# Two value row blocks placed behind the first scores, later divisions by the last sums, casts of outputs in other half heads, and an earlier table request, in a two-layer encoder on one core

## The chip, the cores and the metric

The program runs on one core of one Trainium2 chip. The metric is the device time of one execution in microseconds (us). A core has one queue of instructions for each engine: TensorE (PE, matrix products; PEld is its weight load), VectorE (DVE), ScalarE (ACT), GpSimd (POOL) and SyncE (SP, which only issues DMA transfers). Each engine works through its own queue in order, and a semaphore holds an instruction until what it needs is there.

## The reference, cut to what matters

Two layers, 1,024 positions, 1,024 channels. Each layer joins 8-head latent attention (512 channels) and a convolution branch (512 channels), multiplies both by `w_o`, adds the residual, and then runs a gated feed-forward part with a 3-tap convolution.

```
def _mla_attention(q_nope, q_rope, k_nope, k_rope, v):
    ...
        sc = (jnp.einsum("bqhd,bkhd->bhqk", qn, k_nope)
              + jnp.einsum("bqhr,bkr->bhqk", qr, k_rope))
        p = jax.nn.softmax(sc.astype(jnp.float32) * scale, axis=-1).astype(v.dtype)
        return jnp.einsum("bhqk,bkhd->bqhd", p, v)
...
        kv = (c_kv @ w_ukv[l].astype(h.dtype)).reshape(b, s, MLA_HEADS, MLA_NOPE_DIM + MLA_V_DIM)
        v = kv[..., MLA_NOPE_DIM:]
        y_attn = _mla_attention(q_nope, q_rope, k_nope, k_rope, v)
        ...
        u = jax.nn.silu(_layernorm(u, g_conv_ln[l], b_conv_ln[l]))
        y = jnp.concatenate([y_attn, u], axis=-1) @ w_o[l].astype(h.dtype)
        x = x + y
```

The change touches the attention of each layer: how `v` is made at its start, and how the outputs of the heads are divided by the softmax's sums, split and multiplied by `w_o` at its end.

## The kernel before, in words

Numbers that need more than half precision are kept as a high and a low half (names ending in h and l), and a product is three products of halves. `attention` (L1821) runs once in each layer. Its work comes in **pairs**: 8 heads x 8 blocks of 128 queries, two blocks to a pair, 32 pairs in a layer, numbered 0 to 31. In a name such as `s_0_2` the first number is the head, the second the query block; `t_7_22` is head 7, pair 2 of that head, column group 2.

- **Values.** `rows(tt)` (L1830) makes row block `tt` (0 to 7) of `v`: six matmuls into one PSUM bank `pv`, then `rows_end` (L1839): two ACT copies and two DVE operations that write the high and the low half. Before the loop, the kernel makes blocks 0 to 3 (`ROWS_FIRST`), then the first scores, then 4 and 5, then 6 and 7.
- **Scores.** `scores` (L1851) makes the two score tiles of a pair: four matmuls of the first tile, four short ones with the rotary part `kq` for both, four of the second. `again` (L2051) copies the rotary queries once more, for those short matmuls; it runs once for each head.
- **Softmax.** `largest` (L1875, DVE) takes the negative maximum `mx` of a score tile; `expo` (L1882, ACT) takes the exponential `p` and its sum. Its first call loads a function table (ACT_TABLE_LOAD) that the operations ahead of it did not need.
- **Turning.** `turn` (L1898) transposes `p` on PE in four groups of 4 matmuls, each into a bank `t`; `upper` (L1912, ACT) and `lower` (L1915, DVE) write the high and low half, `pt`.
- **Outputs.** `values` (L1919) and `values_end` (L1935) multiply `pt` by `v` into a bank `o`, two pairs (a half head) at a time; ACT and DVE add the two halves of `o` into `yt`. Pairs with an even number hold `values`' part with 6 matmuls, odd ones the end of a half head.

PSUM has two wide tiles for scores (and for `po_e`) and four banks that `pv`, `t`, `o` and `rc` share, so that a matmul group waits until an older tile's last reader is done. In the loop each pair writes the next pair's scores between the transposes of this one, so PE, ACT and DVE go round in one cycle.

An **agenda** holds side work by its time in half pairs: `others(n)` (L2038) runs what is due. `sums(h)` (L1955) inverts a head's sums, writes them to memory (`sd`) and reads them back spread over the partitions (`rb`); POOL multiplies `yt` by `rb`, and `ys.append(self.split(...))` then casts the product to `ys_1h`, `ys_3h`, `ys_5h` on ACT (a CAST of 128x1024) and makes the low half on POOL. `SUMS_AT`, `Y_DELAY`, `Y_SPLIT` and `Y_LAST` are these times. For the last head the sums are inverted on DVE (`inverse`, L1973) and spread by four transposes on PE into a bank `rc_0s` or `rc_1s` (`spread`, L1978), and DVE divides (L1981). Head 6's outputs are multiplied by `rb` on DVE, in two parts at the times `LAST_MULT`.

At the end of the attention the first products with `w_o` are made early: `early(0, ...)` (L1984) is nine matmuls `po_e` over three pairs of heads, in the order high x high, low x high, high x low. The weights `wo` are loaded by POOL's DMA queue (L1002); `complete` (the dictionary `ahead`, L989) writes the high half of one block on ACT (128x512), and POOL then issues a DMA that forms its low half (L214), 256 KB each. Beside this, POOL adds up the convolution for the layer norm (`lns`, L2173), and SP's queue holds the loads of the residual `y`, issued behind the sums' transfers.

Of the kernel before, what the change touches and what calls it, by code (L numbers as in the profile page):

```python
# [64 lines left out]
FFN_BANKS = (2, 4)  # L65
SIDE_TIME = 56
TOTAL_TIME = 57
Y_DELAY = 5
SUMS_AT = 8
Y_LAST = 4  # L70
Y_SPLIT = 8
LATE_FROM = 0
LAST_MULT = (61, 62)
WO_AT = 55
END_TURNS = 1
SCALES_AT = 2, 4.2
# [3 lines left out]
WO_LOWER = (3, 4), (4, 2), (5, 2), (6, 2)  # L80
P_SCALE = 32768.0
EXPONENT = 8388608.0
ROWS_FIRST, ROWS_SECOND, ROWS_THIRD = (0, 1, 2, 3), (4, 5), (6, 7)
# [66 lines left out]
class Encoder:  # L150
# [421 lines left out]
    def project(self, l, carry):  # L572
# [229 lines left out]
        def query(j):  # L802
            n = self.blk(f"qn{l}_{j}")
            nc.vector.tensor_tensor(out=by_parity(n), in0=in_order(ps[f"n{j}"]), in1=in_order(st["rq"]), op=ALU.mult)  # L804
            hl = self.blk(f"qns{l}_{j}", F16, (128, 2, T))
            nc.scalar.copy(out=hl[:, 0], in_=n)
# [177 lines left out]
    def layer(self, l, carry):  # L984
        with self.psum(f"mix{l}", ([f"w{i}" for i in range(3)], 1), 2):
            mixed = self.project(l, carry)
        with self.psum(f"attn{l}", 2, 4):
            casts, ready = {}, {}
            ahead = {WO_AT: lambda: [casts.update({m: self.wo_cast(l, m, 1)}) for m in range(4)],  # L989
                     **{58 + m: lambda m=m: ready.update({(1, m): self.complete(*casts.pop(m))}) for m in range(3)},  # L990
                     61: lambda: (ready.update({(1, 3): self.complete(*casts.pop(3))}), [casts.update({m: self.wo_cast(l, m, 1)}) for m in range(4, 8)])}
# [829 lines left out]
    def attention(self, l, u, conv, away, spill, kvs, loaded, ahead, wo, begun):  # L1821
# [156 lines left out]
        def spread(c, r):  # L1978
            inv[c], = self.spread(r, f"rc{l}_{c}", HALVES[0:1], self.bank)
# [48 lines left out]
        for c, when in enumerate((60, 62)):  # L2028
            agenda[when].append(lambda c=c: inv.update({c: inverse(c)}))
            agenda[when + 1].append(lambda c=c: spread(c, inv.pop(c)))  # L2030
# [20 lines left out]
        def again(h):  # L2051
            qc = loaded[h][2]
            nc.scalar.copy(out=qc[NOPE:128], in_=qc[0:NOPE])

        for tt in ROWS_FIRST:
            rows(tt)()
        again(0)
        begin(0)
        after[0].pop(0)()
        ends = [rows(tt) for tt in ROWS_SECOND]  # L2060
# [12 lines left out]
        for pair in range(total // 2 - 1):  # L2073
            n, nxt = 2 * pair + 1, pair + 1
            group, odd = divmod(pair - 2, 2)
            if odd and group >= 0:
# [8 lines left out]
            upper(pair, 0)  # L2085
            upper(pair, 1)
            largest(2 * nxt)
            turn(pair, 3)
            lower(pair, 0)
            after[nxt].pop(0)()  # L2090
# [1 line left out]
            upper(pair, 3)  # L2092
            if not odd and group >= 0:
                values(group, 2)
            expo(2 * nxt)
            others(n)
            turn(pair, 2)
            lower(pair, 1)
# [9 lines left out]
            if pair % 4 == 2 and pair // 4 + 1 < HEADS:  # L2108
                again(pair // 4 + 1)
        values_end(2 * HEADS - 2, total - 2)  # L2110
        pair = total // 2 - 1
        early(0, range(3))
        for c in range(4):
            turn(pair, c)
            upper(pair, c)
# [194 lines left out]
```

## Time and profile before

| | us |
|---|---|
| median of 3 runs | 2190.38 (2188.40 to 2190.59) |
| the profiled execution, its own time | 2192.46 |
| span of the profile of that execution | 2190.7 |
| PE busy / DVE busy / ACT busy / POOL busy | 2157.8 / 1839.9 / 1471.1 / 540.4 |
| mean granted clock of PE | 0.998 |

The profile lists instructions by engine with start and duration in us from the span's start; in square brackets stands the idle time ahead of an instruction and what ended it. An entry such as x4 is a run of four like instructions. Matmuls overlap: the next starts before the one ahead of it is over, so work is measured here from start to start. The attention runs from about 202 to 409 us in the first layer and from about 1287 to 1496 us in the second.

### The profile page before, as it was taken

The page shows a single profiled execution, that of the slowest core. Times are in us where ns is not written, and L with a number is a line of the kernel's source. Part 1 is how long each engine was busy: PE and PEld are TensorE (multiplying, and loading weights), DVE is VectorE, ACT ScalarE, POOL GpSimd, SP SyncE. Part 2 cuts the span into 40 slices and gives each one's busy share as a digit, 9 for nine tenths or more (in the row PEclk, how much of TensorE's full clock was granted, in tenths as well). Part 3 has the DMA queues.
Part 4 walks back from the last instruction along what each step waited for, and adds up shares of the span by engine and source line. Part 5 has one row for each costly group of instructions (what it writes and reads, how often), then busy time and mean ns, then how long its engine had stood idle before and what let it go on. Part 6 is the DMA issues. An engine that isn't in the chain of part 4 may idle for free.

```text
span 2190.7 us, 30030 instructions
## 1 busy us (share of the span) xinstructions
PE 2157.8 (98%) x10708; PEld 1245.1 (57%) x10708; DVE 1839.9 (84%) x2531; ACT 1471.1 (67%) x2199; POOL 540.4 (25%) x534
## 2 busy tenths in 40 slices
PE   9999999999999999999999999999999999999998
PEld 7887555654444444644488865557544444446445
DVE  6988998779998887787859789987898988878877
ACT  6365888646898886554623658886468888865544
POOL 1233767211121111000012257570111111110000
PEclk9999999999999999999999999999999999999999
DMA  6898878855689896554578978686646988856533
GB/s 193 181 192 200 168 168 170 248 141 117 142 241 260 224 260 155 192 169 153 167 179 163 186 195 172 144 196 191 168 106 149 258 242 242 242 141 220 182 117 121
DMA packets 170759, 402.81 MB, mean 184 GB/s; under 512 B 25585, under 2 KB 34801, under 8 KB 170609
## 3 DMA queue, kind: packets, MB, share of 16 engines
q0 software_dynamic: 62528, 145.89, 36.4%
q1 hardware_dynamic: 107792, 254.47, 34.1%
q8 instruction: 84, 1.38, 0.3%
q14 instruction: 67, 0.54, 0.1%
q10 hardware_dynamic: 288, 0.53, 0.1%
HBM read 272.46 MB, written 67.56 MB: 155 GB/s over the span
## 4 chain that ended last, share of the span: by engine, by line
PE 87%; ACT 6%; DVE 4%; issue 2%; DMA 1%; SPq 0%; DVEq 0%; ACTq 0%
PE p L1326 36%; PE pd L1571 18%; PE po L1046 7%; PE pq L250 3%; PE pa L250 3%; PE t L1905 3%; ACT p L1887 2%; PE s L1862 2%; PE pkv L250 2%; PE pg L250 2%; PE o L1932 2%; DVE mx L1879 2%; PE pn L250 1%; PE pg L569 1%; ACT pt L1913 1%
## 5 line engine op out<-in xcount | busy, mean ns | idle before, releaser
L1326 PE MATMUL p<-b,w 128*128 128x512 f16 x3696 | 800.1, 379 | 0.3
L1326 PEld LDWEIGHTS <-w 128*128 128x128 f16 x3696 | 358.4, 98 | 432.4 <-DVE w L1290 0.9
L1571 PE MATMUL pd<-ab,wd 128*128 128x512 f16 (+2 forms) x1920 | 404.2, 373 | 0.0
L1216 POOL DMA_DIRECT2D wu<-in_w_up x176 | 152.1, 878 | 772.5 <-DVE w L1290 582.6
L1571 PEld LDWEIGHTS <-wd 128*128 128x128 f16 x1656 | 161.7, 98 | 179.5 <-issue 0.5
L1290 DVE SCALAR_TENSOR_TENSOR w<-wu,wf,w 128x512 f16<-128x512 f32 (+1 forms) x216 | 177.2, 834 | 3.6 <-ACT w L1287 3.6
L1917 DVE SCALAR_TENSOR_TENSOR pt<-t,pt 128x512 f16<-128x512 f32 x256 | 164.2, 679 | 10.7 <-ACT pt L1913 10.3
L1913 ACT ACTIVATE pt<-t 128x512 f16<-128x512 f32 x256 | 144.2, 596 | 40.3 <-PE t L1905 39.5
L1879 DVE TENSOR_REDUCE mx<-s 128x1 f32<-128x1024 f32 x128 | 155.9, 1218 | 13.8 <-PE s L1869 11.3
L1287 ACT ACTIVATE w<-wu,wf 128x512 f16<-128x512 f32 (+1 forms) x216 | 164.8, 781 | 0.0
L1905 PE MATMUL t<-ident,p 128*128 128x128 f32 x1024 | 151.3, 278 | 11.0 <-ACT p L1887 6.0
L1887 ACT ACTIVATE p<-s,mx 128x1024 f32<-128x1024 f32 x128 | 142.5, 1113 | 17.0 <-DVE mx L1879 15.4
L1905 PEld LDWEIGHTS t<-ident,p 128*128 128x128 f32 x1024 | 118.0, 141 | 55.2 <-issue 12.8
L1560 ACT ACTIVATE ab<-ac,ds 128x512 f16<-128x512 f32 x108 | 75.5, 716 | 108.7 <-DVE ac L1475 75.2
L2162 POOL TENSOR_SCALAR late<-gate,par 128x1019 f32<-128x1019 f32 (+13 forms) x99 | 136.4, 1377 | 29.5 <-DVE qn L804 15.3
L2145 DVE SCALAR_TENSOR_TENSOR conv<-gate,par,conv 128x1009 f32<-128x1009 f32 (+14 forms) x110 | 139.8, 1274 | 3.0 <-ACT conv L664 0.4
L1862 PE MATMUL s<-k,q 128*128 128x512 f16 x512 | 131.8, 380 | 2.3 <-ACT p L1887 2.3
L1786 DVE SCALAR_TENSOR_TENSOR o<-zg,par,o 128x1023 f32<-128x1023 f32 x88 | 112.8, 1281 | 8.8 <-ACT o L1780 7.4
L1334 DVE SCALAR_TENSOR_TENSOR zg<-p,wf,zg 128x512 f32<-128x512 f32 x72 | 54.0, 750 | 71.3 <-PE p L1326 61.7
L1786 DVE SCALAR_TENSOR_TENSOR v<-zv,par,v 128x1023 f32<-128x1023 f32 x88 | 112.1, 1276 | 0.0
L1561 DVE SCALAR_TENSOR_TENSOR ab<-ac,ds,ab 128x512 f16<-128x512 f32 x108 | 79.8, 747 | 19.2 <-ACT ab L1560 19.2
L1232 ACT ACTIVATE wsq<-wu 128x1024 f16<-128x1024 f32 x88 | 92.0, 1046 | 0.0
(2180 smaller groups left out, 3797.6 us busy)
## 6 DMA issues: line engine op xcount, KB each, us to landing
wu<-in_w_up SPq DMA_DIRECT2D x98, 512.0 KB, 4.6
wu<-in_w_up POOLq DMA_DIRECT2D x176, 256.0 KB, 4.9
sd<-in_w_down SPq DMA_DIRECT2D x44, 512.0 KB, 7.4
ws<-sd SPq DMA_DIRECT2D x44, 512.0 KB, 5.5
act<-v SPq DMA_DIRECT2D x36, 512.0 KB, 4.6
ac<-act SPq DMA_DIRECT2D x72, 256.0 KB, 5.1
wo<-in_w_o POOLq DMA_DIRECT2D x32, 256.0 KB, 7.5
x_mix<-y SPq DMA_DIRECT2D x32, 256.0 KB, 3.6
```

What stands on the lines that cost most here:

```text
L250: nc.tensor.matmul(ps[:, HALVES[c]], w, x[:, HALVES[c]], start=(k == 0 and s == 0), stop=(k == n - 1 and s == 2))
L1287: nc.scalar.activation(out=t, in_=src, func=AF.Copy, scale=scale[f])
L1290: nc.vector.scalar_tensor_tensor(out=t, in0=src, scalar=scale[f], in1=hi, op0=ALU.mult, op1=ALU.subtract)
L1326: nc.tensor.matmul(ps, w[p][:, k * 128:(k + 1) * 128], b[:, q], start=(i in (1, 5, 2) and k == 0 and t == 0), stop=(k == 3 and t == 2), sk ...
L1571: nc.tensor.matmul(ps[t, m][:, cs], w[i, j][p][:, m * 128:(m + 1) * 128], b[:, q, cs], start=(i in (1, 5, 2) and j == 0 and s == 0), stop= ...
L1786: self.nc.vector.scalar_tensor_tensor(out=o[:, a:b], in0=z[:, at + a:at + b], scalar=self.par[l][:, tap:tap + 1], in1=o[:, a:b], op0=ALU.m ...
L1862: nc.tensor.matmul(two[e][:, cs], q[:, i, at[e]], k[:, i, cs], start=(i == 0 and e == 0), stop=(i == 1 and e == 1), skip_group_check=True)
L1879: nc.vector.tensor_reduce(out=mx, in_=st["s"][qt], op=ALU.max, axis=AX.X, negate=True)
L1887: nc.scalar.activation(out=p, in_=ps, func=AF.Exp, bias=mx, accum_out=st["sums"][:, qt:qt + 1])
L1905: nc.tensor.transpose(tp[:, i, qi * 128:(qi + 1) * 128], st["p"][2 * qp + qi][:, kt * 128:(kt + 1) * 128], self.ident)
L1913: nc.scalar.activation(out=halves(pair, c)[0], in_=tps[pair, c], func=AF.Copy, scale=P_SCALE)
L1917: nc.vector.scalar_tensor_tensor(out=lo, in0=tps.pop((pair, c)), scalar=P_SCALE, in1=hi, op0=ALU.mult, op1=ALU.subtract)
```

## The change

Five things move; no arithmetic on the data is added or left out. ACT gets one new instruction for each layer, an exponential of one column of ones (128x1).

- Row block 3 of `v` goes behind the first scores; blocks 6 and 7 go into pairs 0 and 1 of the loop.
- The copy `again` runs ahead of the first value blocks for head 0, and one step earlier in the loop for the others. The one-column exponential, which needs the same table, stands ahead of the last cast of the queries (`qns_3`).
- The sums of a head are inverted one pair later, POOL's multiplication comes one half pair earlier on the agenda, and the casts `ys_1h` and `ys_3h` move from odd pairs (15, 23) to even ones (16, 24), `ys_5h` from pair 29 to pair 28.
- The four high halves of `wo_10` to `wo_13` are written by two agenda entries, at 60 and 61, and no longer one at a time at 58 to 61.
- `rc_0s` is spread behind the first nine `po_e` matmuls, `rc_1s` behind the last transposes, and the two DVE multiplications of head 6 move from 61 and 62 to 63 and 64.

```
@@ -65,12 +65,12 @@
 FFN_BANKS = (2, 4)
 SIDE_TIME = 56
 TOTAL_TIME = 57
-Y_DELAY = 5
-SUMS_AT = 8
-Y_LAST = 4
-Y_SPLIT = 8
+Y_DELAY = 4
+SUMS_AT = 10
+Y_LAST = 3
+Y_SPLIT = 11
 LATE_FROM = 0
-LAST_MULT = (61, 62)
+LAST_MULT = (63, 64)
 WO_AT = 55
 END_TURNS = 1
 SCALES_AT = 2, 4.2
@@ -80,7 +80,7 @@
 WO_LOWER = (3, 4), (4, 2), (5, 2), (6, 2)
 P_SCALE = 32768.0
 EXPONENT = 8388608.0
-ROWS_FIRST, ROWS_SECOND, ROWS_THIRD = (0, 1, 2, 3), (4, 5), (6, 7)
+ROWS_FIRST, ROWS_SECOND, ROWS_THIRD, ROWS_LATE = (0, 1, 2), (3,), (4, 5), (6, 7)
 E = mybir.EngineType
 MANUAL = [E.PE, E.DVE, E.Activation, E.Pool, E.SP]
 LATE_KINDS = (("pool", "both", "pool", "pool", "pool"), ("pool", "both", "pool", "pool", "pool"))
@@ -803,6 +803,8 @@
             n = self.blk(f"qn{l}_{j}")
             nc.vector.tensor_tensor(out=by_parity(n), in0=in_order(ps[f"n{j}"]), in1=in_order(st["rq"]), op=ALU.mult)
             hl = self.blk(f"qns{l}_{j}", F16, (128, 2, T))
+            if j == 3:
+                nc.scalar.activation(out=self.cp.tile([128, 1], F32, name=f"table{l}", tag="table", bufs=1), in_=self.ones[:, 0:1], func=AF.Exp)
             nc.scalar.copy(out=hl[:, 0], in_=n)
             yield 1.22, 1.5
             nc.vector.scalar_tensor_tensor(out=hl[:, 1], in0=n, scalar=1.0, in1=hl[:, 0], op0=ALU.mult, op1=ALU.subtract)
@@ -987,8 +989,9 @@
         with self.psum(f"attn{l}", 2, 4):
             casts, ready = {}, {}
             ahead = {WO_AT: lambda: [casts.update({m: self.wo_cast(l, m, 1)}) for m in range(4)],
-                     **{58 + m: lambda m=m: ready.update({(1, m): self.complete(*casts.pop(m))}) for m in range(3)},
-                     61: lambda: (ready.update({(1, 3): self.complete(*casts.pop(3))}), [casts.update({m: self.wo_cast(l, m, 1)}) for m in range(4, 8)])}
+                     60: lambda: [ready.update({(1, m): self.complete(*casts.pop(m))}) for m in range(2)],
+                     61: lambda: [ready.update({(1, m): self.complete(*casts.pop(m))}) for m in range(2, 4)]
+                     + [casts.update({m: self.wo_cast(l, m, 1)}) for m in range(4, 8)]}
             begun_scales = lambda: self.more_scales(l, mixed[4][3])
             begun = {"x": {}, "po": {}}
             begun["turn"] = lambda: ready.update({(1, m): self.complete(*casts.pop(m)) for m in range(4, 4 + END_TURNS)})
@@ -2025,9 +2028,9 @@
         for h in range(HEADS - 1):
             agenda[SUMS_AT + 8 * h].append(lambda h=h: sums(h))
         agenda[60].append(lambda: [self.load_y(l, begun["x"], 0, k) for k in range(2)])
-        for c, when in enumerate((60, 62)):
+        for c, when in enumerate((60, 63)):
             agenda[when].append(lambda c=c: inv.update({c: inverse(c)}))
-            agenda[when + 1].append(lambda c=c: spread(c, inv.pop(c)))
+        agenda[64].append(lambda: spread(1, inv.pop(1)))
         self.last_pair = lambda: finish(last, state_y(), 1)
         for i in range(1, 4):
             agenda[TOTAL_TIME + i - 1].append(lambda i=i: self.conv_total(l, conv, i))
@@ -2052,9 +2055,9 @@
             qc = loaded[h][2]
             nc.scalar.copy(out=qc[NOPE:128], in_=qc[0:NOPE])
 
+        again(0)
         for tt in ROWS_FIRST:
             rows(tt)()
-        again(0)
         begin(0)
         after[0].pop(0)()
         ends = [rows(tt) for tt in ROWS_SECOND]
@@ -2073,6 +2076,7 @@
         for pair in range(total // 2 - 1):
             n, nxt = 2 * pair + 1, pair + 1
             group, odd = divmod(pair - 2, 2)
+            ends = [rows(ROWS_LATE[1])] if pair == 1 else []
             if odd and group >= 0:
                 values_end(group, n)
             elif group >= 0:
@@ -2085,6 +2089,8 @@
             upper(pair, 0)
             upper(pair, 1)
             largest(2 * nxt)
+            for f in ends:
+                f()
             turn(pair, 3)
             lower(pair, 0)
             after[nxt].pop(0)()
@@ -2092,7 +2098,12 @@
             upper(pair, 3)
             if not odd and group >= 0:
                 values(group, 2)
+            ends = [rows(ROWS_LATE[0])] if pair == 0 else []
             expo(2 * nxt)
+            for f in ends:
+                f()
+            if pair % 4 == 2 and pair // 4 + 1 < HEADS:
+                again(pair // 4 + 1)
             others(n)
             turn(pair, 2)
             lower(pair, 1)
@@ -2105,11 +2116,10 @@
             others(n + 1)
             for qi in range(2):
                 state[pair // 4]["p"].pop(2 * (pair % 4) + qi)
-            if pair % 4 == 2 and pair // 4 + 1 < HEADS:
-                again(pair // 4 + 1)
         values_end(2 * HEADS - 2, total - 2)
         pair = total // 2 - 1
         early(0, range(3))
+        spread(0, inv.pop(0))
         for c in range(4):
             turn(pair, c)
             upper(pair, c)
```

On DVE, at the start of the first layer's attention: `v` rows are the low halves of value blocks (their `pv` number is the row block), `mx` the maxima, `pt` the low halves of turned probabilities. Before:

```order
L1848 SCALAR_TENSOR_TENSOR v_2_1653<-pv_3_1658,sc_85,v_2_1653 128x4x64 x2
L1879 TENSOR_REDUCE mx_0_0_1695<-s_0_0_1671 128x1
L1848 SCALAR_TENSOR_TENSOR v_4_1703<-pv_4_1681,sc_85,v_4_1703 128x4x64 x2
L1848 SCALAR_TENSOR_TENSOR v_4_1703<-pv_5_1688,sc_85,v_4_1703 128x4x64 x2
L1879 TENSOR_REDUCE mx_0_1_1712<-s_0_1_1672 128x1
L1848 SCALAR_TENSOR_TENSOR v_6_1730<-pv_6_1714,sc_85,v_6_1730 128x4x64 x2
L1848 SCALAR_TENSOR_TENSOR v_6_1730<-pv_7_1721,sc_85,v_6_1730 128x4x64 x2
L1879 TENSOR_REDUCE mx_0_2_1765<-s_0_2_1739 128x1
L1917 SCALAR_TENSOR_TENSOR pt_10_1760<-t_0_00_1745,pt_00_1759 128x2x256
L1879 TENSOR_REDUCE mx_0_3_1777<-s_0_3_1740 128x1
L1917 SCALAR_TENSOR_TENSOR pt_10_1760<-t_0_01_1754,pt_00_1759 128x2x256
L1917 SCALAR_TENSOR_TENSOR pt_11_1762<-t_0_02_1788,pt_01_1761 128x2x256
```

After the change:

```order
L1851 SCALAR_TENSOR_TENSOR v_2_1656<-pv_2_1649,sc_85,v_2_1656 128x4x64 x2
L1882 TENSOR_REDUCE mx_0_0_1679<-s_0_0_1662 128x1
L1851 SCALAR_TENSOR_TENSOR v_2_1656<-pv_3_1672,sc_85,v_2_1656 128x4x64 x2
L1882 TENSOR_REDUCE mx_0_1_1691<-s_0_1_1663 128x1
L1851 SCALAR_TENSOR_TENSOR v_4_1709<-pv_4_1693,sc_85,v_4_1709 128x4x64 x2
L1851 SCALAR_TENSOR_TENSOR v_4_1709<-pv_5_1700,sc_85,v_4_1709 128x4x64 x2
L1882 TENSOR_REDUCE mx_0_2_1744<-s_0_2_1718 128x1
L1920 SCALAR_TENSOR_TENSOR pt_10_1739<-t_0_00_1724,pt_00_1738 128x2x256
L1882 TENSOR_REDUCE mx_0_3_1756<-s_0_3_1719 128x1
L1851 SCALAR_TENSOR_TENSOR v_6_1768<-pv_6_1759,sc_85,v_6_1768 128x4x64 x2
L1920 SCALAR_TENSOR_TENSOR pt_10_1739<-t_0_01_1733,pt_00_1738 128x2x256
L1920 SCALAR_TENSOR_TENSOR pt_11_1741<-t_0_02_1779,pt_01_1740 128x2x256
```

The first maximum now stands behind three value blocks and the second behind one more; the block 6 stands behind the fourth maximum, and the block 7 (not shown) behind the fifth.

On POOL, at the end of that attention: the adds `lns` of the convolution, the low half `ys_5l`, and the DMAs that form the low halves of `wo_10` to `wo_13`. Before:

```order
L2173 TENSOR_TENSOR lns_3778<-conv_0_477,conv_1_541 128x1024
L214 DMA wo_10_3703<-in_w_o 128x512
L2173 TENSOR_TENSOR lns_3778<-lns_3778,conv_2_719 128x1024
L214 DMA wo_11_3705<-in_w_o 128x512
L2173 TENSOR_TENSOR lns_3778<-lns_3778,conv_3_856 128x1024
L234 TENSOR_TENSOR ys_5l<-yt_4_2998,ys_5h 128x1024
L214 DMA wo_12_3707<-in_w_o 128x512
L214 DMA wo_13_3709<-in_w_o 128x512
```

After the change:

```order
L2183 TENSOR_TENSOR lns_3777<-conv_0_477,conv_1_541 128x1024
L234 TENSOR_TENSOR ys_5l<-yt_4_3000,ys_5h 128x1024
L2183 TENSOR_TENSOR lns_3777<-lns_3777,conv_2_719 128x1024
L2183 TENSOR_TENSOR lns_3777<-lns_3777,conv_3_856 128x1024
L214 DMA wo_10_3706<-in_w_o 128x512
L214 DMA wo_11_3708<-in_w_o 128x512
L214 DMA wo_12_3710<-in_w_o 128x512
L214 DMA wo_13_3712<-in_w_o 128x512
```

The DMAs for `wo_10` and `wo_11` stood between the adds, and now all four stand behind them.

On PE, at the last pairs: `o_7_0` is the output bank of the last head's first half, `rc_0s` the spread inverse sums, `t_7_22` a group of transposes. Before:

```order
L1932 MATMUL o_7_0_3859<-pt_01_3755,v_4_1703 128x512
L327 MATMUL rc_0s<-ident,rc_0_3872 128x128 x4
L1905 MATMUL t_7_22_3939<-ident,p_7_4_3841 128x128 x2
L1905 MATMUL t_7_22_3939<-ident,p_7_5_3857 128x128 x2
L1944 LDWEIGHTS v_0_1630
L1944 MATMUL o_7_0_3859<-pt_10_3754,v_0_1630 64x512
```

After the change:

```order
L1935 MATMUL o_7_0_3857<-pt_01_3754,v_4_1709 128x512
L1908 MATMUL t_7_22_3935<-ident,p_7_4_3845 128x128 x2
L1908 MATMUL t_7_22_3935<-ident,p_7_5_3855 128x128 x2
L1947 LDWEIGHTS v_0_1633
L1947 MATMUL o_7_0_3857<-pt_10_3753,v_0_1633 64x512
```

The four transposes of `rc_0s` are gone from this place (they stand behind the ninth `po_e` matmul now), so `t_7_22` takes the bank that they took.

More of the change, by code (lines that the diff above doesn't have):

```diff
@@ L67 @@
 TOTAL_TIME = 57
[L68 to L71, printed above, removed]
+Y_DELAY = 4
+SUMS_AT = 10
+Y_LAST = 3
+Y_SPLIT = 11
 LATE_FROM = 0
-LAST_MULT = (61, 62)
+LAST_MULT = (63, 64)
 WO_AT = 55
@@ L82 @@
 EXPONENT = 8388608.0
[L83 removed]
+ROWS_FIRST, ROWS_SECOND, ROWS_THIRD, ROWS_LATE = (0, 1, 2), (3,), (4, 5), (6, 7)
 E = mybir.EngineType
@@ L805, in query @@
             hl = self.blk(f"qns{l}_{j}", F16, (128, 2, T))
+            if j == 3:
+                nc.scalar.activation(out=self.cp.tile([128, 1], F32, name=f"table{l}", tag="table", bufs=1), in_=self.ones[:, 0:1], func=AF.Exp)
             nc.scalar.copy(out=hl[:, 0], in_=n)
@@ L989, in layer @@
             ahead = {WO_AT: lambda: [casts.update({m: self.wo_cast(l, m, 1)}) for m in range(4)],
-                     **{58 + m: lambda m=m: ready.update({(1, m): self.complete(*casts.pop(m))}) for m in range(3)},
-                     61: lambda: (ready.update({(1, 3): self.complete(*casts.pop(3))}), [casts.update({m: self.wo_cast(l, m, 1)}) for m in range(4, 8)])}
+                     60: lambda: [ready.update({(1, m): self.complete(*casts.pop(m))}) for m in range(2)],
+                     61: lambda: [ready.update({(1, m): self.complete(*casts.pop(m))}) for m in range(2, 4)]
+                     + [casts.update({m: self.wo_cast(l, m, 1)}) for m in range(4, 8)]}
             begun_scales = lambda: self.more_scales(l, mixed[4][3])
@@ L2053, in again @@
             nc.scalar.copy(out=qc[NOPE:128], in_=qc[0:NOPE])
+        again(0)
         for tt in ROWS_FIRST:
             rows(tt)()
-        again(0)
         begin(0)
@@ L2075, in attention @@
             group, odd = divmod(pair - 2, 2)
+            ends = [rows(ROWS_LATE[1])] if pair == 1 else []
             if odd and group >= 0:
@@ L2087, in attention @@
             largest(2 * nxt)
+            for f in ends:
+                f()
             turn(pair, 3)
@@ L2094, in attention @@
                 values(group, 2)
+            ends = [rows(ROWS_LATE[0])] if pair == 0 else []
             expo(2 * nxt)
+            for f in ends:
+                f()
+            if pair % 4 == 2 and pair // 4 + 1 < HEADS:
+                again(pair // 4 + 1)
             others(n)
@@ L2107, in attention @@
                 state[pair // 4]["p"].pop(2 * (pair % 4) + qi)
-            if pair % 4 == 2 and pair // 4 + 1 < HEADS:
-                again(pair // 4 + 1)
         values_end(2 * HEADS - 2, total - 2)
@@ L2112, in attention @@
         early(0, range(3))
+        spread(0, inv.pop(0))
         for c in range(4):
```

4 lines of the change are left out of this document (2 added, 2 removed).

## The prediction

> **What bounds the kernel now.** I read the page's engine table first, then the largest group of PE's waits by releaser, then the windows of the first layer's attention.
>
> ```profile
> PE 2157.8 (98%) x10708; PEld 1245.1 (57%) x10708; DVE 1839.9 (84%) x2531; ACT 1471.1 (67%) x2199; POOL 540.4 (25%) x534
> ...
> PE o L1932 <- DVE pt L1917: 8.6, 22, 0.5
> ...
> 204.00:222.00 18.00, 15.26 (x85) 9.78 (x84) 13.70 (x24) 13.69 (x27) 15.81 (x14) 1.00 1.00 233
> 222.00:385.00 163.00, 157.56 (x1023) 92.53 (x1021) 147.57 (x192) 143.88 (x253) 119.57 (x98) 1.00 0.81 170
> 385.00:409.00 24.00, 19.88 (x108) 13.34 (x107) 17.26 (x26) 14.80 (x26) 12.33 (x13) 0.93 1.07 351
> ```
>
> PE is busy for 98% of the span. The wait row gives total us, times and the longest; a window's row gives its length, the busy time of PE, PEld, DVE, ACT and POOL, then PE's granted clock, the DMA share and GB/s. PE idles 2.74 us of 18 at the start, 5.44 of 163 in the middle and 4.12 of 24 at the end, there at a clock of 0.93. No PE work goes, so the change can win only from these about 12 us for each layer, and loses wherever it opens new waits.
>
> **The start.** The first two views are DVE's and ACT's instructions by time, the third PE's.
>
> ```profile
> 202.84 3.22 DVE L1848 SCALAR_TENSOR_TENSOR v<-pv,sc,v 128x256 f16<-128x256 f32 x8
> 205.97 1.21 DVE L1879 TENSOR_REDUCE mx<-s 128x1 f32<-128x1024 f32 x1
> 209.19 1.66 DVE L1848 SCALAR_TENSOR_TENSOR v<-pv,sc,v 128x256 f16<-128x256 f32 x4 [2.00 <-ACT v L1845]
> 210.76 1.22 DVE L1879 TENSOR_REDUCE mx<-s 128x1 f32<-128x1024 f32 x1
> ...
> 215.56 1.22 DVE L1879 TENSOR_REDUCE mx<-s 128x1 f32<-128x1024 f32 x1
> ```
>
> ```profile
> 200.62 1.05 ACT L806 CAST qns<-qn 128x1024 f16<-128x1024 f32 x1 [2.48 <-DVE qn L804]
> 201.57 3.02 ACT L1845 ACTIVATE v<-pv,sc 128x256 f16<-128x256 f32 x8
> 204.61 0.62 ACT L2053 COPY kq<-kq 64x512 f16<-64x512 f16 x1
> 205.25 1.28 ACT L1887 ACT_TABLE_LOAD   x1
> 207.22 1.12 ACT L1887 ACTIVATE p<-s,mx 128x1024 f32<-128x1024 f32 x1 [0.69 <-DVE mx L1879]
> ...
> 208.32 1.56 ACT L1845 ACTIVATE v<-pv,sc 128x256 f16<-128x256 f32 x4
> ...
> 218.53 1.11 ACT L1887 ACTIVATE p<-s,mx 128x1024 f32<-128x1024 f32 x1
> ```
>
> ```profile
> 201.83 0.39 PE L1835 MATMUL pv<-wv0h,kvs_0h 128*128 128x512 f32 x1
> ...
> 203.19 1.04 PE L1862 MATMUL s<-k,q 128*128 128x512 f16 x4
> 204.16 0.39 PE L1869 MATMUL s<-kq 32*128 32x512 f16 x1
> 205.28 0.49 PE L1869 MATMUL s<-kq 32*128 32x512 f16 x3 [0.74 <-ACT kq L2053]
> ...
> 219.79 0.44 PE L1905 MATMUL t<-ident,p 128*128 128x128 f32 x2 [0.49 <-ACT p L1887]
> ...
> 222.28 0.60 PE L1905 MATMUL t<-ident,p 128*128 128x128 f32 x4
> 222.72 1.46 PE L1932 MATMUL o<-pt,v 128*128 128x512 f16 x6
> ```
>
> The steps read from these: maximum to exponential 1.25 (205.97 to 207.22); exponential to ACT's next 1.10; ACT's copy of a value block to DVE's part of it 0.87 (208.32 to 209.19), and 0.79 for a block on DVE (two in 209.19 to 210.76); exponential to the transposes that read it 1.26 (218.53 to 219.79); four transposes 0.44 (222.28 to 222.72), four score matmuls 0.97 (203.19 to 204.16). A value block is 1.36 on PE (201.83 to 203.19), 0.23 a matmul; four short ones are about 0.4.
>
> *The table and the copy.* The exponential waits 0.69 for the maximum behind the load's 1.28, so an earlier load wins nothing by itself; its new place is ACT's idle 2.48 ahead of the last query cast. The copy `kq` (0.62) now precedes the value copies and removes PE's wait of 0.74, which is beside the DVE chain; it pushes ACT's first value copy to 202.19 and DVE's to 203.06, 0.2 later. I take 0 for both beyond that, bounds -0.7 to +0.3. [...]
>
> *The maxima.* Three blocks stand ahead of the first maximum instead of four: 205.97 - 0.78 + 0.2 = 205.4. Then exponential 206.65, ACT's block 3 at 207.75, DVE's at 208.62, second maximum 209.40 (before 210.76), exponential 210.65, blocks 4 and 5 on DVE at 212.62, third maximum 214.19 (before 215.56): 1.4 earlier.
>
> *PE.* Before, blocks 6 and 7 filled PE while the second exponential was awaited. Now PE starts block 0 to 2 where it did, has the first scores at 201.83 in the place of block 3, and is through block 5, the first half of the next scores and half a group of transposes at about 209.35 and idles until 210.65 + 1.26 = 211.91: **2.56**. `t_0_03` then waits for a bank that block 4 holds until 213.41: 0.4. Block 6 runs at 214.8 to 216.2, `t_0_02` to 216.6. Block 7 takes block 6's bank, and that is read late: ACT's copy stands behind the third exponential (215.44 + 1.10), DVE's follows at 217.41 and ends at 218.2: **1.6** idle. Block 7 ends at 219.6, the next scores, transposes and short matmuls at 221.8. ACT's copy of block 7 stands behind two upper halves (222.8), DVE's part ends at 224.3, and `t_0_12` waits for it 0.9 or more. The first `o` follows at 224.8, where it stood at 222.72: **+2.1**. The earlier maximum is spent there, since the next scores come only behind block 7. The loop behind it idles little (5.44 in 163), so nothing is caught up. Two layers: +4.2. Bounds for a layer: -1.4 (the third maximum's gain is carried on whole) to +2.7 (all of the first gap).
>
> **The casts.** View: ACT's and PE's instructions in pair 15.
>
> ```profile
> 302.77 1.03 ACT L232 CAST ys_1h<-yt 128x1024 fp32r<-128x1024 f32 x1
> ...
> 305.46 0.44 PE L1905 MATMUL t<-ident,p 128*128 128x128 f32 x2 [0.57 <-ACT p L1887]
> ```
>
> In an odd pair the cast costs PE 0.57 of its 0.94 (start to the next start). In an even pair PE already waits 22 times for the turned lower halves (the wait row), so ACT and DVE are the bound there and up to all 0.94 counts. The difference is at most 0.37; I take 0.27, and four casts (two in each layer) give **+1.1**, bounds -2.3 (hidden whole) to +1.5. The later sums delay POOL's product and SP's later loads by some 5 us; POOL is busy 25%, and I take 0. The other copies `again` only change places with an exponential or an upper half on a busy ACT: 0.
>
> **The end.** Views: PE, DVE and ACT by time, the windows of the slow clock, the DMA issues in two short windows, and the page's row for another transfer of that size.
>
> ```profile
> 387.17 0.44 PE L1905 MATMUL t<-ident,p 128*128 128x128 f32 x2 [1.21 <-ACT p L1887]
> ...
> 390.09 0.60 PE L327 MATMUL rc_0s<-ident,rc 128*128 128x128 f32 x4
> 392.81 0.63 PE L1905 MATMUL t<-ident,p 128*128 128x128 f32 x4 [2.12 <-DVE pt L1917]
> ...
> 394.38 0.80 PE L1046 MATMUL po_e<-ys_1h,wo 128*128 128x512 f32 x1
> ...
> 407.60 0.47 PE L2189 MATMUL lnp<-lns0h,ones_r 128*128 128x512 f32 x1 [0.79 <-DVE yt L1982]
> ...
> 391.00 1.06 DVE L1966 SCALAR_TENSOR_TENSOR yt<-yt,rb 64x512 f32<-64x512 f32 x1
> ...
> 387.00 0.63 ACT L213 ACTIVATE wo<-wo 128x512 fp32r<-128x512 f32 x1
> ...
> 394.00:395.00 1.00, 1.00 (x6) 0.53 (x3) 0.90 (x2) 1.00 (x3) 0.57 (x2) 0.63 1.10 363
> 395.00:396.00 1.00, 1.00 (x4) 0.81 (x3) 1.00 (x3) 0.84 (x3) 0.00 (x0) 0.50 1.10 256
> 396.00:397.00 1.00, 1.00 (x4) 0.81 (x3) 0.97 (x2) 0.00 (x0) 0.00 (x0) 0.50 1.11 268
> 397.00:398.00 1.00, 1.00 (x4) 0.75 (x4) 0.24 (x1) 0.00 (x0) 0.00 (x0) 0.67 1.10 256
> ...
> wo<-in_w_o POOLq DMA_DIRECT2D x1, 256.0 KB, 6.3
> ...
> wo<-in_w_o POOLq DMA_DIRECT2D x1, 256.0 KB, 8.1
> ...
> wu<-in_w_up POOLq DMA_DIRECT2D x176, 256.0 KB, 4.9
> ```
>
> *What goes.* `t_7_22` waits 2.12 because `rc_0s` took the bank ahead of it, and the bank left is read behind the 1.06 multiplication. With both moved, the wait goes. Right behind it the clock falls to 0.50 for some 3.4 us; the missing clock of the four windows is 0.37 + 0.50 + 0.50 + 0.33 = 1.70. Together **-3.82** a layer. The 1.21 wait goes with the cast and one copy `wo`; the cast costs its 0.94 in pair 28, and two copies stand behind the exponential: 0 net, bounds -0.6 to +0.3.
>
> *What is late next.* The third `po_e` matmul is the first to read a low half of `wo`. PE comes to it sooner: `t_7_22` at 390.09, the first `po_e` 1.57 later (394.38 - 392.81), the third 0.45 behind (two steps of 0.23): 392.1. But the copy of `wo_10` now runs where that of `wo_12` ran, at 387.00, and the DMA for its low half is issued behind it at 387.7 (later yet if POOL's adds last longer). At 6.3 to 8.1 it lands at 394.0 to 395.8: a new wait of **1.9 to 3.7**, for which the old one was cover. A wait of 2.12 brought the half clock, so this one may: 0 to 1.7, I take 0.6. The two multiplications now stand between the last lower halves and the division for which PE waits 0.79 already: 0 to 2.1, I take 0.9. Sum: -3.82 + 2.8 + 0.6 + 0.9 = about **+0.4** a layer, bounds -1.9 to +3.7 by these rows; +0.8 in two.
>
> **The clock at the start.** The 2.56 gap is longer than the 2.12 that brought the half clock; 3.4 us at 0.50, partly idle anyway, cost about 1 a layer. I count 0.7 for the two, bounds 0 to 3.4. [...]
>
> **The sum.** 4.2 + 1.1 + 0.8 + 0.7 = +6.8. On the profiled execution's own 2192.46 that is 2199.3; the median of the runs lies 2.1 lower, at 2190.38, which gives **2197.2**.
>
> **The rivals.** *The low halves land early.* These DMAs were issued under a DMA share of 1.07; the residual's loads beside them now come later. If one lands in 4.9, as the page's median row for another 256 KB transfer of POOL's queue says, the wait is 0.5, the clock stays full, and the end gives -3.82 + 0.5 + 0.9 = -2.4 a layer: 4.2 + 1.1 - 4.8 = +0.5, 2190.9. Against it: the rows of these very transfers are 6.3 and 8.1. *Faster.* Place: the same low half; landing within 4.4 us of its issue leaves no wait at all, and the multiplications hide beside PE: -3.8 a layer, -7.6 in all. It decides once the start costs under about 0.5 a layer; with the start at 0 it gives -7.6 + 1.1 = -6.5, 2183.9. Against it: the gaps at the start need no estimate of a transfer. *Clock lost twice.* Start gap and end wait both bring the half clock in both layers, at a landing of 8.1: 4.2 + 1.1 + 2 x 1.0 + 2 x 2.2 = +11.7, 2202.1.
>
> **How the numbers follow.** Forecast 0.41, low halves early 0.33, faster 0.12, clock lost twice 0.14. A measurement tells 0.2% (4.4 us) from no change. Forecast and clock case are slower (0.55), the early landing is within (0.33), the faster case 0.12. The range 2187.5 to 2204 leaves out most of the faster case and the end of the clock's. The forecast's own range is 2194.8 to 2200.
>
> **What would show it.** Right: in the changed profile the first `o` of the attention about 2 us later, a PE wait near 2.5 ahead of the first transposes and one near 1.6 at block 7; no 2.12 wait at `t_7_22`, but a wait of `po_e` for a DMA of `wo`. Wrong: `po_e` runs through without a wait, the clock at the end stays at 1.00, or the first `o` comes at 223 or before; even pairs with a cast no longer than the others would void that term.

## The result, and the profile after

The changed kernel takes 2206.01 us (median of 4 runs, 2204.88 to 2206.67) against 2190.49 for the kernel before: 15.5 us slower, a ratio of 1.0072 with a 95% interval of 1.0054 to 1.0089. The direction was forecast and the mechanisms are in the trace, but the time lies above the range (2187.5 to 2204.0). The profiled execution's own time is 2205.38, its span 2203.6.

The waits of PE in the changed kernel by releaser (total us, times, longest):

```profile
PE t L1908 <- ACT p L1890: 11.6, 22, 2.4
PE po_e L1049 <- DMA wo<-in_w_o: 7.2, 2, 3.7
PE o L1935 <- DVE pt L1920: 4.5, 13, 0.4
PE pv L1838 <- DVE v L1851: 3.0, 2, 1.5
PE lnp L2199 <- DVE yt L1985: 2.9, 2, 1.4
PE t L1908 <- DVE v L1851: 2.6, 3, 1.1
```

Before, none of the second and fourth rows' waits existed, and the longest in the first row was 1.2. The second row is a transfer: 3.6 a layer. PE at the start of the first layer's attention, in the changed kernel:

```profile
196.51 0.39 PE L1838 MATMUL pv<-wv0h,kvs_0h 128*128 128x512 f32 x1
...
210.71 0.44 PE L1908 MATMUL t<-ident,p 128*128 128x128 f32 x2 [2.44 <-ACT p L1890]
...
218.78 0.47 PE L1838 MATMUL pv<-wv0h,kvs_0h 128*128 128x512 f32 x1 [1.49 <-DVE v L1851]
...
225.05 0.63 PE L1908 MATMUL t<-ident,p 128*128 128x128 f32 x4 [1.12 <-DVE v L1851]
```

These are the three gaps of the forecast (2.56, 1.6, 0.9) at their places. DVE's third maximum is where it was forecast, too:

```profile
212.99 1.22 DVE L1882 TENSOR_REDUCE mx<-s 128x1 f32<-128x1024 f32 x1
```

That is 16.48 behind the first value block, where it stood 17.81 behind it (215.56 less 197.75): 1.3 earlier. The windows behind the first gap and behind the wait for the transfer (length, busy times of PE to POOL, then PE's clock, DMA share, GB/s):

```profile
212.00:213.00 1.00, 0.62 (x4) 0.59 (x4) 1.00 (x4) 1.00 (x3) 0.87 (x2) 0.59 1.16 225
213.00:214.00 1.00, 1.00 (x5) 0.56 (x4) 1.00 (x2) 0.52 (x2) 1.00 (x2) 0.50 1.05 196
214.00:215.00 1.00, 1.00 (x4) 0.49 (x2) 0.80 (x2) 0.92 (x2) 0.70 (x2) 0.50 0.95 175
215.00:216.00 1.00, 1.00 (x5) 0.79 (x4) 0.73 (x1) 0.45 (x2) 1.00 (x2) 0.71 1.10 208
...
399.00:400.00 1.00, 1.00 (x4) 0.87 (x5) 0.00 (x0) 0.00 (x0) 0.00 (x0) 0.95 1.11 262
400.00:401.00 1.00, 1.00 (x4) 0.71 (x4) 0.00 (x0) 0.00 (x0) 0.00 (x0) 0.50 1.11 262
401.00:402.00 1.00, 1.00 (x5) 0.80 (x4) 0.00 (x0) 0.00 (x0) 0.00 (x0) 0.50 1.11 262
402.00:403.00 1.00, 1.00 (x7) 1.00 (x6) 0.00 (x0) 0.00 (x0) 0.00 (x0) 0.50 1.11 262
403.00:404.00 1.00, 1.00 (x8) 0.96 (x7) 0.04 (x1) 0.67 (x2) 0.00 (x0) 0.84 1.10 270
```

The missing clock adds up to 1.70 in the first four windows and to 1.71 in the last five. PE runs at half clock twice in a layer, where the profile of the kernel before has it once (0.50 in 395.00 to 397.00, and in 1480.00 to 1482.00 of the second layer). Then PE at the end, ACT's copies of the weights, POOL's issue, and the row of the first of these issues in the DMA view (KB, us to landing). The copy in `complete` (L213) writes the negative of the high half into the low half's tile, and the DMA then adds the weight to it; where this document says that a high half is written, it means this copy.

```profile
393.06 0.60 PE L1908 MATMUL t<-ident,p 128*128 128x128 f32 x4
...
398.99 0.50 PE L1049 MATMUL po_e<-ys_1h,wo 128*128 128x512 f32 x1 [3.68 <-DMA wo<-in_w_o]
...
407.11 1.04 PE L1935 MATMUL o<-pt,v 128*128 128x512 f16 x4 [0.60 <-DVE yt L1985]
...
413.74 0.47 PE L2199 MATMUL lnp<-lns0h,ones_r 128*128 128x512 f32 x1 [1.45 <-DVE yt L1985]
...
389.99 1.14 ACT L213 ACTIVATE wo<-wo 128x512 fp32r<-128x512 f32 x2
...
390.91 1.83 POOL L214 DMA_DIRECT2D wo<-in_w_o  x2 [0.87 <-ACT wo L213]
...
wo<-in_w_o POOLq DMA_DIRECT2D x1, 256.0 KB, 8.0
```

`t_7_22` (393.06) no longer waits, and the third early output matmul waits 3.68 for the low half of `wo_10`, issued at 390.91 and landed 8.0 later (7.9 in the second layer). Before, that DMA went out at 380.45 and landed 6.3 later, at 386.7, ahead of the first early output matmul (394.38):

```profile
380.45 0.91 POOL L214 DMA_DIRECT2D wo<-in_w_o  x1 [2.34 <-ACT wo L213]
```

The division comes later too, and PE waits 0.60 and 1.45 for it.

A table by stage makes every run comparable: from the first value block to the first output matmul ("start"), on to the first early output matmul ("middle"), and on to the first full output product behind the layer norm's matmuls ("end"). The stretch from there to the second layer's first value block is 874.9 to 875.0 in every run of this study.

| | start | middle | end |
|---|---|---|---|
| before, layer 1 / 2 | 24.97 / 25.18 | 171.66 / 172.19 | 14.24 / 13.73 |
| after | 29.05 / 28.64 | 169.02 / 168.93 | 20.17 / 20.01 |
| difference | +4.08 / +3.46 | -2.64 / -3.26 | +5.93 / +6.28 |

Together +13.85, where the two profiled executions differ by 12.9 (the first attention starts 1.24 earlier in the changed kernel, and the stretch behind the second is 0.3 longer).

### The profile page after: what moved, and what is told of

Read it like the earlier page. It is cut to its first block, busy times and chain, and to the rows that moved or that the text cites. A ratio compares the mean times of both kernels' runs of the same rounds, so it can differ in the third digit from the quotient of the medians.

```text
span 2203.6 us, 30033 instructions
## 1 busy us (share of the span) xinstructions
PE 2160.7 (98%) x10708; PEld 1243.2 (56%) x10708; DVE 1841.7 (84%) x2531; ACT 1473.6 (67%) x2201; POOL 540.8 (25%) x534
## 5 line engine op out<-in xcount | busy, mean ns | idle before, releaser
L1908 PE MATMUL t<-ident,p 128*128 128x128 f32 x1024 | 157.1, 282 | 14.2 <-ACT p L1890 11.6
```

What stands on the lines that cost most here:

```text
L1908: nc.tensor.transpose(tp[:, i, qi * 128:(qi + 1) * 128], st["p"][2 * qp + qi][:, kt * 128:(kt + 1) * 128], self.ident)
```

## The experiments

**One: the row blocks back.** The changed kernel with

```
+ROWS_FIRST, ROWS_SECOND, ROWS_THIRD = (0, 1, 2, 3), (4, 5), (6, 7)
-            ends = [rows(ROWS_LATE[1])] if pair == 1 else []
-            ends = [rows(ROWS_LATE[0])] if pair == 0 else []
```

> The changed kernel with the value row blocks placed as before (0 to 3 ahead of the first scores, 4 to 7 ahead of the loop), all else changed. Theory: the changed start costs 4.1 and 3.5 us in the two layers (first value block to first output matmul 29.05 and 28.64 against 24.97 and 25.18), so the time falls by about 7.5 to 2198.5, the gaps of 2.4 and 1.5 go, and the end keeps its wait of about 3.6 for the weights' low halves. Rival (the early table request and copy, or the end, carry most of the loss): the time stays above 2203.

Measured: 2197.56 (ratio to before 1.0031, 1.0019 to 1.0044). Start 25.39 / 25.19, end 20.11 / 19.67. The blocks' places, with the half clock that they bring beside the early copy, cost over half of the loss; the rival falls.

**Two: the row blocks alone**, the same lines the other way round, put into the kernel before.

> The kernel before with only the value row blocks moved; the copy for the rotary queries, the table, the casts and the end stay. Theory: slower by about 7.5, 2198; the gaps at the start as in the changed kernel, with half clock behind the first. Rival (the start only loses together with the early copy and table): within 2 of before.

Measured: 2194.67 (1.0009 to 1.0026 times before): 4.2 slower, not 7.5. Start 27.30 / 27.50, and PE's gaps in the first layer are

```profile
203.47 0.49 PE L1869 MATMUL s<-kq 32*128 32x512 f16 x3 [1.40 <-ACT kq L2053]
...
210.62 0.44 PE L1905 MATMUL t<-ident,p 128*128 128x128 f32 x2 [0.35 <-ACT p L1887]
...
217.16 0.47 PE L1835 MATMUL pv<-wv0h,kvs_0h 128*128 128x512 f32 x1 [1.50 <-DVE v L1848]
...
211.00:215.00 4.00, 3.62 (x23) 2.56 (x23) 3.67 (x7) 3.44 (x7) 3.61 (x4) 1.00 1.01 198
```

The old place of the rotary copy splits the first gap into 1.40 and 0.35 (0.59 and 1.34 in the second layer), and the clock (last row, a window) stays at 1.00. The blocks cost 2.3 a layer by waits; the other 1.1 to 1.8 come only with the rest of the change. This is neither of the two outcomes written down, and led to runs six and seven.

**Six: the rotary copy back at the start**, all else as changed.

```
-        again(0)
         for tt in ROWS_FIRST:
             rows(tt)()
+        again(0)
```

> The changed kernel with the first copy of the rotary queries behind the first value row blocks, as before; all else changed. Theory (the clock): the copy's wait splits the start's idle time into about 1.4 and 0.4, so that the clock stays at 1.00 and a start is 27.4 in place of 29.05 and 28.64: 2.9 faster, 2203. Rival (the idle time itself is the cost, whatever its place): the start stays at 28.6 to 29 and the time at 2206.

**Seven: the gap filled.** The changed kernel, with more work on PE. The output doesn't change, as the second pass writes the same tile anew.

```
-            whole(0)
+            for _ in range(2 if pair == 1 else 1):
+                whole(0)
```

> The changed kernel with the four matmuls of the first half of pair 1's scores done twice, just ahead of the gap of 2.44 (0.87 more of PE's work a layer, with no effect on the output). Theory (the clock): the gap shrinks to about 1.6, the clock stays at 1.00 behind it and a start is about 27.5: 2 to 3 faster though PE has more to do. Rival (no clock effect): the start stays at 28.6 to 29, the time at 2206 or above.

Measured: six 2203.26 (1.0050 to 1.0075), seven 2203.71 (1.0048 to 1.0074). Starts 27.33 / 27.52 and 27.65 / 27.51. The same window of the changed kernel, of six and of seven, in that order:

```profile
212.00:216.00 4.00, 3.62 (x13) 2.43 (x13) 3.54 (x6) 2.88 (x6) 3.57 (x4) 0.57 1.06 201
```

```profile
212.00:216.00 4.00, 3.62 (x23) 2.45 (x24) 3.30 (x6) 3.44 (x8) 3.70 (x4) 1.00 1.01 199
```

```profile
211.69 0.44 PE L1909 MATMUL t<-ident,p 128*128 128x128 f32 x2 [1.74 <-ACT p L1891]
...
212.00:216.00 4.00, 3.62 (x24) 2.53 (x23) 3.60 (x7) 3.44 (x7) 3.41 (x4) 1.00 1.02 200
```

Seven has eight matmuls more in the two layers, and its median is 2.3 below that of the changed kernel. All five of its executions (2202.95 to 2204.78) are below all four of the changed kernel's (2204.88 to 2206.67), but the intervals of six and seven against the kernel before overlap with the changed kernel's, so the stages carry the verdict: starts shorter by 1.1 to 1.7. Nearly all of it lies behind the gap: from the first transposes that end it to the first output matmul it is 14.85 and 14.45 in the changed kernel, 13.32 and 13.33 in six, 13.29 and 13.31 in seven. The gap of 2.44 became 1.74, and the half clock (0.57 as a mean of the window, 13 matmuls in it where the others have 23 and 24) was gone. So part of the start's price is the clock, and an edit that looked harmless (the early copy, which removes a wait of 0.74) brought it about by joining two gaps (1.41 and 0.34 in run six) into one of 2.44.

**Three: the weights early.** The changed kernel with

```
-                     60: lambda: [... for m in range(2)],
-                     61: lambda: [... for m in range(2, 4)]
+                     **{58 + m: lambda m=m: ready.update({(1, m): self.complete(*casts.pop(m))}) for m in range(3)},
+                     61: lambda: (ready.update({(1, 3): self.complete(*casts.pop(3))}), ...
```

> The changed kernel with the four high halves of the output weights written one at a time at 58 to 61, as before. Theory: the wait of the early output products for a DMA (3.7 and 3.5) goes, and with it the half clock behind it (1.7 a layer): 2206 - 7.2 - 3.4 = about 2195.5; the added waits at the last division (0.6 and 0.65 a layer) stay. Rival (the division chain sets the end, so the wait was beside it): 2 to 3 us faster at most.

Measured: 2197.15 (1.0017 to 1.0040): 8.9 faster than the changed kernel. Middle 169.97 / 169.91, end 14.65 / 14.63. No wait for a transfer is left; the clock of the window 395 to 399 is 1.00, and the waits for the division remain:

```profile
402.19 1.04 PE L1934 MATMUL o<-pt,v 128*128 128x512 f16 x4 [0.66 <-DVE yt L1984]
408.83 0.47 PE L2198 MATMUL lnp<-lns0h,ones_r 128*128 128x512 f32 x1 [1.44 <-DVE yt L1984]
```

The 1.6 by which it missed the expectation is about what the middle lost: it is 1.0 a layer longer with the copies one at a time.

**Four: the multiplications back**, `LAST_MULT = (61, 62)` in the changed kernel.

> The changed kernel with head 6's two multiplications at 61 and 62, as before. Theory: only the two added waits at the division (0.60 ahead of the last head's outputs, 0.66 more ahead of the layer norm's matmul) go: 2.5 faster, 2203.5; the wait for the weights stays at about 3.6, and the wait of 2.12 doesn't come back, since the transposes no longer read the bank behind the multiplication. Rival (the multiplication's old place alone made the 2.12): the 2.12 comes back in front of the DMA wait, which shrinks by as much, and the time stays.

Measured: 2204.02 (1.0045 to 1.0070): 2.0 faster by the medians; the intervals overlap, and the ends, 1.6 and 1.3 shorter, carry the verdict. End 18.57 / 18.75; the wait for the transfer stays (3.52 and 3.69), the wait ahead of the outputs is gone, that at the layer norm is 0.79 again, and no 2.12 comes back, so the rival falls.

**Eight: only `rc_0s` later**, in the kernel before.

```
         early(0, range(3))
+        spread(0, inv.pop(0))
```

> The kernel before with nothing but rc_0s spread behind the first nine early output matmuls. Theory: the wait of 2.12 and the half clock behind it (1.70) go, for 0.4 more of rc_0s later and a wait or two of some tenths: 2 x 3 less, 2184.5. Rival (what was beside the wait is late next, the weights' low halves or the division): 2188 or more with a new wait at the early output matmuls.

Measured: 2186.11 (0.9972 to 0.9990), 4.2 below the kernel before. Middle 168.92 in both layers, end 14.30 / 13.94, clock 1.00 throughout. The 2.12 is gone; two smaller waits are late next, at `rc_1s` and at the layer norm:

```profile
394.22 0.65 PE L327 MATMUL rc_1s<-ident,rc 128*128 128x128 f32 x4 [0.58 <-DVE yt L1948]
...
403.31 0.47 PE L2190 MATMUL lnp<-lns0h,ones_r 128*128 128x512 f32 x1 [1.15 <-DVE yt L1982]
```

**Ten: both spreads later**, in the kernel before: as in eight, and `rc_1s` from its agenda time to 64, its inverse to 63.

> The kernel before with the later places of both spreads (rc_0s behind the ninth early output matmul, rc_1s behind the last transposes) and nothing else. Theory: as with rc_0s alone, and the wait of 0.58 at rc_1s goes too, with some tenths at the last division: a layer's end is 12.3 in place of 13.3, so 2 faster than that run: 2184. Rival (the 0.58 only turns up at the next wait for the division): 2186.

Measured: 2183.14 (0.9960 to 0.9981), the fastest of all: by the medians 7.7 us under the kernel before (4.2 to 8.8 by the interval) and 23 under the changed one. End 12.83 / 12.98, which is 1.5 and 1.0 shorter than in eight; the expectation's 12.3 and 13.3 are not ends of this table, but its difference of 1.0 is. PE's two waits that are left around its end, first layer:

```profile
385.80 0.44 PE L1905 MATMUL t<-ident,p 128*128 128x128 f32 x2 [1.21 <-ACT p L1887]
402.51 0.47 PE L2190 MATMUL lnp<-lns0h,ones_r 128*128 128x512 f32 x1 [0.33 <-DVE yt L1982]
```

**Twelve: ten, with the weights two at a time at 60 and 61.**

> The kernel with both spreads later, and the weights' high halves written two at a time at 60 and 61 as in the change; nothing else. Theory: the wait of the third early output matmul for the DMA is there by this edit alone, about 3.5, with half clock behind it: 2 x (3.5 + 1.7) more than with the spreads alone, less what the copies' old places cost: about 2193.5. Rival (the wait needs the later sums, whose transfers delay the loads on the queues): 2188 or less.

Measured: 2191.02 (0.9990 to 1.0008): 7.9 slower than ten. The wait is there by this edit alone (3.06 and 3.36), with no later sums in the kernel:

```profile
394.02 0.79 PE L1047 MATMUL po_e<-ys_1h,wo 128*128 128x512 f32 x1 [3.06 <-DMA wo<-in_w_o]
```

End 18.93 / 17.97, 6.1 and 5.0 longer than in ten; the middle, 167.92 / 167.93, is 1.0 shorter, which is the main reason that the loss is below the 10.4 of the expectation. The stages make it 9.1 and not 7.9: the profiled execution, 2192.88, is the slowest of the eleven, and in its first layer PE's steps are those of the half clock (0.42 to 0.43 for an early output matmul, 0.23 at full clock) from the end of the wait at 394.02 to about 400.1, in the second from about 1482.2 to 1485.4.

**Five: all of the end's gains.** The changed kernel with the edits one, three, four and six together.

> The changed kernel with four things back: the value row blocks and the first copy of the rotary queries as before, the weights' high halves at 58 to 61, head 6's multiplications at 61 and 62. What stays of the change: the later spread of rc_0s and rc_1s, the casts in even half heads, the copies in the loop, the early table. Theory: the start is that of before (25.0), the wait of 2.12 and the half clock behind it are gone and nothing takes their place: by the parts of the runs so far a layer loses 1.26 against before (changed kernel with early weights, less its start) and 1.3 more for the multiplications, 5.1 in all: about 2185.5. Rival (the late spread only moves a wait to the end of the last head): 2189 or more.

Measured: 2186.10 (0.9970 to 0.9988). Start 25.00 / 25.20, middle 169.90 / 169.87, end 12.82 in both. It has the end of ten, and its middle is 0.9 longer: with the casts and copies where the change puts them, the middle does not gain, it loses (runs nine and eleven).

**Nine: the sums and casts alone**, in the kernel before (`Y_DELAY`, `SUMS_AT`, `Y_LAST`, `Y_SPLIT` as changed).

> The kernel before with only the times of the sums, products and casts changed (sums a pair later, casts ys_1h and ys_3h in even half heads, ys_5h a pair earlier). Theory of the prediction: +1.1 to +1.5 (an even half head pays 0.85 to 0.94 for a cast where an odd one paid about 0.66). Rival (the casts are hidden in either place, or the 1.21 wait that the moved ys_5h removes pays for them): within 0.5 of before, or faster.

Measured: 2190.60, a ratio of 0.9993 to 1.0011: no difference that this can tell (-1.5 to +2.4 us). The forecast +1.1 is inside. The stages are finer: the middle is 172.04 / 171.96 at a clock of 1.00, against 171.66 in the first layer of the kernel before (the 172.19 of its second has half clock in it), so the casts cost about 0.35 a layer there.

**Eleven: the early table and the copies alone**, in the kernel before.

> The kernel before with only the early one-column exponential (the table) and the earlier copies of the rotary queries, at the start and in the loop. Theory: within 1 of before: the load was beside the wait for the maximum, the copy's wait of 0.74 turns into a wait of about 1.4 ahead of the first transposes, and each copy in the loop only changes places on a busy engine. Rival (the table hides 1.3 or more a layer): 2.6 faster or better.

Measured: 2191.15, 0.9993 to 1.0011. ACT loads the table ahead of the last cast, the one-column exponential follows right behind the load, and ACT then waits longer for the same maximum:

```profile
198.44 1.28 ACT L807 ACT_TABLE_LOAD   x1
199.73 0.20 ACT L807 ACTIVATE table<-ones_r 128x1 f32<-128x1 f32 x1
...
207.88 1.11 ACT L1889 ACTIVATE p<-s,mx 128x1024 f32<-128x1024 f32 x1 [2.23 <-DVE mx L1881]
```

The wait was 0.69 behind the load; it is 2.23 without it. The rival (2.6 faster) falls. By the stages the copies in the loop are not free: the middle of the second layer, at a clock of 1.00, is 172.31, about 0.65 longer than before. With the 0.35 of the casts that is the 0.9 by which five's middle is longer than ten's.

## Why the prediction was wrong, point by point

| step of the prediction, both layers | forecast | measured |
|---|---|---|
| waits at the start | +4.2 | +4.65 (run two, clock 1.00) |
| half clock behind the first gap | +0.7 | +2.8 (starts of the changed kernel less those of six) |
| table, copies | 0 | not told from 0 by the medians of run eleven; about +1.3 by its middle |
| casts | +1.1 | not told from 0 by the medians of run nine; about +0.7 by its middle |
| middle and end together, with the casts and copies | +1.9 | +6.3 (the stage table) |

The mechanisms stood as written: the gaps of 2.44, 1.49 and 1.12, the third maximum 1.3 earlier and the gain spent ahead of block 7, the 2.12 gone, and a wait for the low half of `wo_10` in its place. The terms that failed are sizes. By the stages the start is 2.6 above its forecast (7.5 against 4.9), and the middle and end are 4.4 above theirs. Over half of this, 4.3, is one step: **the half clock was discounted by hand**, to 0.6 a layer behind the new wait and to 0.35 a layer behind the first gap, where the runs show 1.7 and 1.1 to 1.7. The next is the new wait itself. Both stand in **the sum of the end, +0.4 a layer** (by its own terms it is 0.48).

- *The new wait* was put at 2.8, the middle of 1.9 to 3.7, and is 3.68 and 3.52. The transfers took 8.0 and 7.9 from issue to landing, at the upper row (8.1), and I had taken the middle of both rows: 1.6 in two layers. The lower row, 6.3, was this transfer at its early place, the upper one the next transfer, issued at 384.89. The runs' traces separate the two places: issued early, the transfer for `wo_10` lands in 4.1 to 6.3 (the kernel before and runs two, three, five, eight, nine, ten and eleven); issued where the change puts it, in 7.4 to 8.3 (the changed kernel and runs one, four, six, seven and twelve). The later sums are not the reason, as run nine has them and lands in 4.1 and 4.2, and twelve lacks them and lands in 7.4 and 7.7. Why a later issue lands later stays open.
- *The clock behind it* was put at 0.6 and was 1.7: half clock in both layers of the profiled execution, with the windows at 0.50 shown above. The prediction has "so this one may", though a shorter wait had brought the half clock in the trace that it quoted. This is 2.2 in two layers. Even the upper bound, 1.7, was too low: of the twelve waits for this transfer in six profiles (3.06 to 3.90 long), eight lose 1.7 to 1.8 by the clock and four 2.3 to 3.0 (runs one, six, seven and twelve, in one layer each): from the third early output matmul to the eleventh PE takes 4.86 to 4.91 in the eight and 5.49 to 6.13 in the four, against 3.15 in run three, at full clock and without a wait.
- *The clock that goes* was counted at its full 1.70 a layer. The medians had only part of it: of the 67 executions of the kernel before beside the experiments, 18 show a mean clock of 1.000 (mean time 2189.3), 30 of 0.999 (2190.4) and 19 of 0.998 (2192.4), and the profiled one, 2192.46, was of the last. Run nine keeps the 2.12 and shows clock 1.00 behind it in its profile:

```profile
391.56 0.63 PE L1905 MATMUL t<-ident,p 128*128 128x128 f32 x4 [2.12 <-DVE pt L1917]
...
391.00:396.00 5.00, 4.44 (x28) 3.25 (x29) 3.52 (x6) 2.46 (x5) 2.33 (x5) 1.00 1.09 304
```

  So against the median about half of the 3.4 was never there to win: the profiled execution lies 2.1 above the median and is of the class with the lowest clock, and the forecast set its whole saving against the median.
- *The multiplications* were put at 0.9 and cost 1.26 (0.60 and the difference of 1.45 and 0.79), by run four 1.0 a layer (medians) to 1.2 and 1.5 (middle and end).
- *The half clock at the start* was halved by hand to 0.7 for two layers. All four executions of the changed kernel have a mean clock of 0.997, and its gap of 2.44 paid in both layers: 1.7 and 1.1.
- *The copies two at a time* were put at 0 and win 1.0 a layer in the middle (run twelve against ten), better than the forecast and beyond the bound of -0.6 of the term it stood in.

Added up for a layer, -2.12 and -1.70 for what goes, +3.6 for the wait, +1.7 for its clock, +1.26 for the multiplications, -1.0 for the copies two at a time and +1.0 for the casts and the copies in the loop make +2.7. The stage table has +3.15; the 0.4 that is left is not assigned.

By the length of the gap, the runs have this: six gaps of 2.43 to 2.61 (the changed kernel, runs three and four) all have half clock behind them (a mean of 0.72 over 211 to 217 in all three, of 0.72, 0.76 and 0.72 behind the second layer's), gaps of 1.74 and 1.57 (run seven) have none (1.00 in 212 to 216 and in 1303 to 1308), and of eight gaps of 2.12 (the kernel before, runs two, nine and eleven) four have it, in runs two and eleven one layer and not the other: the early output matmuls behind the gap then step at 0.43, elsewhere at 0.23.

The rival "low halves land early" needed 4.9 and got 8.0. The one called "clock lost twice" had the right mechanism and was given 0.14; it fell short (2202.1; by its own terms the end is 2.5 a layer and not 2.2, which gives 2202.7), in part as it left the whole clock saving in the sum.

## What to carry to other kernels

Count a transfer backwards from its reader: here the issue moved from 380.45 to 390.91 while the reader was ready at 395.3, and a transfer that had landed in 6.3, unseen, now took 8.0 and became a wait of 3.6. Removing a wait cost time here, as it joined two short gaps of TensorE (1.41 and 0.34, run six) into one of 2.44, with starts longer by 1.7 and 1.1; look at the clock rows behind the longest gap, not only at the sum of idle time. And take a change apart: one of its edits (the later spreads) wins 7.7 us alone by the medians, and others (the blocks with the early copy, the weights two at a time, the multiplications) cost more than that.

## What the runs showed of the hardware that was not expected

The same wait of 2.12 us has half clock behind it in four of its eight places in the profiles and not in the other four, and the kernel before spreads from 2188.2 to 2193.3, the slower executions at the lower mean clock (0.998 at 2192.4, 1.000 at 2189.3, as means). Nor does a wait's length alone tell how long the half clock lasts: behind a wait of 3.06 (run twelve, first layer) PE's steps are those of the half clock for 6.1 us, behind one of 3.82 (run seven, second layer) for 3.3 us. In these profiles, the gap of 2.4 at the start has half clock behind it in both layers of the changed kernel; one of 1.74, and the pair of 1.40 and 0.35, have none. That more matmuls in a gap shorten the stage (28.64 to 29.05 became 27.51 to 27.65, with the clock at 1.00) was forecast for run seven, but nothing in the prediction had counted on it.
